# A diffusion trunk on one Trainium2 core: last tile's evictions on two engines behind the first products' copies, its stores on another queue, block sums split elsewhere and combined on GpSimd

## The chip, the core and the metric

The program runs on one core of a Trainium2 chip. The core has a matrix engine (TensorE, written PE in the profile), a vector engine (VectorE, DVE), a scalar engine (ScalarE, ACT), GpSimd (POOL) and SyncE (SP, which here only issues transfers). Each engine works through its own queue of instructions in order; semaphores order work between engines. Transfers between the chip's memory and the core's on-chip memory (SBUF) are issued from the queues of SP and ACT. Matrix products land in PSUM, from which ACT or DVE copies ("evicts") them.

The metric is the device time of one launch in microseconds. Before the change it was 2740.33 us, the median of three runs that lie between 2739.74 and 2740.53.

## The reference

One trunk layer on 2048 latent tokens of width 1024 (256 context tokens enter only the mixer): a gated recurrence (the mixer), then a gated convolutional feed-forward part, each behind an RMS norm with shift and scale. Cut to what the change touches:

```python
D_MODEL, SEQ, D_FF = 1024, 2048, 2816

def conv_ffn(h, w_up, conv_w, conv_b, w_down):
    u = dwconv(h @ w_up, conv_w, conv_b)           # h: (2048, 1024), w_up: (1024, 5632)
    gate, val = jnp.split(u, 2, axis=-1)
    return (jax.nn.silu(gate) * val) @ w_down

    lat = lat + g1 * yl                            # yl: the mixer's output
    hl = modulate(rmsnorm(lat, norm_g[l, 1]), sh2, sc2)
    lat = lat + g2 * conv_ffn(hl, ffn_w_up[l], ffn_conv_w[l], ffn_conv_b[l], ffn_w_down[l])
    return rmsnorm(lat, final_g)
```

The change lies where the mixer's last rows are normed and the first columns of `h @ w_up` are computed.

## The kernel before

**Numbers.** All data are float32. A matrix that enters a product is first split in two: `split(h, l, src)` has ACT copy the source into a rounded form `h` (line 78) and DVE subtract that from the source, which gives the rest `l` (line 79). A product of two such pairs is computed as high x high, high x low and low x high.

**Block products.** `h @ w_up` is computed with 7 instead of 8 block products (Strassen's scheme in Winograd's form). The tokens are taken in two halves of 8 tiles of 128 rows; half 1 goes first. On the token side stand, for each half, the blocks B11, B21, B22 (inputs), and T1, T2, T3, T4 (differences of blocks); on the weight side A11, A12, A22 and the sums S1 = A21 + A22, S2 = S1 - A11, S3 = A11 - A21, S4 = A12 - S2. Each of the 22 column chunks of a half has a `Pair` object that holds the four weight blocks (two raw loads of 0.5 MB in the buffer `raw`) and their sums. The products are A11 x B11, S2 x T2, S1 x T1, S3 x T3, A12 x B21, S4 x B22, A22 x T4. Each is one call of `acc_mm`: four steps over the inner dimension, three matrix instructions each (lines 1065, 1067, 1068), 12 matrix instructions of 128x128 by 512 columns. The pairs go two by two (`q` = 0, 1), so each kind of product comes as 24 matrix instructions. In the profile the left name is the PSUM tile: `z` for the first pairs' early products, `za`, `zb`, `zc`, `zd` in the main loop; `rB` stands for B11, B21 and B22, `rT` for T1 to T4.

**The products that come early.** `mixer_out` walks through the mixer's 16 tiles backwards (t = 15 to 0). For each it makes the output product and adds it to the latent rows `lat` (line 1209); then `norm_steps` makes the norm: ACT sums the squares (line 1215), DVE and GpSimd make the scale `rs` (lines 74, 75), and DVE applies it, which gives `xn` (line 1218). `norm2` then transposes `xn` on PE (line 120, 8 transposes), evicts the two PSUM tiles `tp` with shift and scale into `hm` (`transpose_mod`: line 124 on ACT, line 127 on DVE), makes the differences of this tile and its neighbour (lines 1256, 1257, 1262) and splits and puts them (`put`). Tiles 8 to 15 (half 1) are split into place or put, tiles 0 to 7 (half 0) are put into chip memory (`rhs0...`) for later. Since half 1 is complete long before tile 0 is done, the first two pairs of half 1 (`first`) are begun in here, so that PE has work while tile 0 is normed: A11 x B11 (result copied to `u2` by ACT, line 1345), A12 x B21 (added to it in PSUM, copied to `ug` by ACT, line 1351) and S2 x T2 (added to `u2` by DVE, line 1366). The rest of these pairs, S1 x T1, S4 x B22, S3 x T3 and A22 x T4, is the start of the main loop. There DVE adds S1 x T1 to `u2`, which gives `uv` (line 1549), S4 x B22 goes onto the same PSUM tile `zd`, and S3 x T3 is added to `uv` (line 1557).

**Weights of the first pairs.** S1 and S2 are made by DVE (`sums`, lines 1132, 1133). Since their buffers are needed again, `sums_in_place` writes S3 and S4 with DVE over A21 and A12 (lines 1139, 1140) and copies S1 with ACT over A11 (line 1141); S1 is split from there. For all later pairs GpSimd makes S1 to S4 (lines 1132, 1133, 1149, 1153; the same line can show on either engine).

**Buffers.** The buffers of T3 and T4 (`rT3`, `rT4`, tiles of 2 MB) lie on memory that the mixer uses up to the transposes of tile 0; they are loaded by SP (line 1108), T3 first. The loads of the next raw weights (line 1095) come behind them in SP's queue. Weight splits go into a ring of 11 buffers; the buffers of two earlier states (`Sf`, `Sb`) serve besides.

**What sets the order.** The program's text gives the order of the calls; a scheduler then sets the order on each engine by priority (text order, unless `tc.high_priority` moves a piece ahead), with ties: `tc.issue_after(i)` holds what is issued inside it behind instruction i, and `behind_of(pair)` behind the two instructions of a split. `prepare(g)` issues the weight splits of the main loop's g-th product ahead of its use; how far ahead is set by the `while ready <= ...` line.

Of the kernel before, what the change touches and what calls it, by code (L numbers as in the profile page):

```python
# [11 lines left out]
F32 = mybir.dt.float32  # L12
F32R = mybir.dt.float32r
# [32 lines left out]
def body(ctx, tc, a, out):  # L46
# [1073 lines left out]
    class Pair:  # L1120
# [14 lines left out]

        def sums_in_place(self):

            v = self.src
            dve.tensor_tensor(v["A21"], v["A11"], v["A21"], OP.subtract)
            dve.tensor_tensor(v["A12"], v["A12"], v["S2"], OP.subtract)  # L1140
            act.activation(v["A11"], v["S1"], AF.Copy)
            self.src = {"S3": v["A21"], "S4": v["A12"], "S1": v["A11"], "A22": v["A22"]}

        def split(self, n, w=None):
            if n in self.w:
                return
            if n == "S3" and n not in self.src:
                s3 = self.src["A21"]
                pool.tensor_tensor(s3, self.src["A11"], s3, OP.subtract)
                self.src[n] = s3  # L1150
            if n == "S4" and n not in self.src:
                s2 = self.src["S2"]
                pool.tensor_tensor(s2, self.src["A12"], s2, OP.subtract)
                self.src[n] = s2
            if w is None:
                w = ring_tile([128, 2, 4, 128])
            split(w[:, 0], w[:, 1], self.src[n])
            self.w[n] = w
# [5 lines left out]
    def mixer_out(c3):  # L1164
# [57 lines left out]
        def put(n, t, src):  # L1222
# [13 lines left out]
            put_split.append(split(w[:, 0], w[:, 1], src))  # L1236
            (sp if t > 1 else act).dma_start(rhs_d[half][n][:, j], w.bitcast(F32))

        def norm2(t, xn, on_act=True):

            hm = wn.tile([128, KT, 128], F32, name="hm", tag="hm", bufs=3)
            for g in range(2):
                transpose_mod(xn, hm, g, ps, A2, B2, "tr", 4, on_act)
            a, b = hm[:, 0:4], hm[:, 4:8]
# [91 lines left out]
        for q, p in enumerate(first):  # L1336
            p.sums(dve, *[pl[1][:, q, i].bitcast(F32) for i in range(2)])
        for q, p in enumerate(first):
            p.split("S2", pl[0][:, 2 + q])
        al = []  # L1340
        for q, p in enumerate(first):
            z = ps.tile([128, HJ, 128], F32, name="z", tag="y")
            multiplied = acc_mm(z, p.w.pop("A11"), rhs["B11"], True)
            u2 = h2p.tile([128, HJ, 128], F32, name="u2", tag="u2", bufs=2)
            act.activation(u2, z, AF.Copy)
            al.append((z, u2))
        for q, p in enumerate(first):
            z, u2 = al[q]
            acc_mm(z, p.w.pop("A12"), rhs["B21"], False)
            ug = u_tile(h2p, "g")  # L1350
            kept = act.activation(cols(ug, 0), z, AF.Copy).ins
            begun.append((u2, ug))
            if q == 0:
                for p in first:
                    p.sums_in_place()
                for p in first:
                    p.split("S1")
        behind.append(tc.cur_priority)
        with tc.issue_after(kept), tc.issue_after(multiplied):
            norm2(0, xn)  # L1360
        for q, p in enumerate(first):
            u2, _ = begun[q]
            z = ps.tile([128, HJ, 128], F32, name="z", tag="oi")
            acc_mm(z, p.w.pop("S2"), rhs["T2"], True)
            with tc.issue_after(put_split[2 * q - 4][1]):
                dve.tensor_tensor(u2, u2, z, OP.add)
# [154 lines left out]

    with tc.high_priority(offset=tc.cur_priority - behind[0]):
        for g in range(4):
            prepare(g)
    ready, added = 4, []
    for g, (half, s, n, q, pairs) in enumerate(todo):
        with ExitStack() as tied:
            for i in added[-1:]:
                tied.enter_context(tc.issue_after(i))
            while ready <= min(g + LOOK, max(2 * g + 3, 5)):  # L1530
                prepare(ready)
                ready += 1
# [332 lines left out]
```

## Time and profile before

| what | value |
|---|---|
| median of three runs | 2740.33 us |
| the profiled execution, its own time | 2739.58 us |
| its span (first to last instruction) | 2737.9 us |
| mean granted TensorE clock | 0.997 |
| busy PE | 2702.6 us, 99% |
| busy DVE | 1978.3 us, 72% |
| busy ACT | 1138.8 us, 42% |
| busy GpSimd | 566.8 us, 21% |
| PE busy from 1485 to 1490 us | 3.84 of 5.00 us |
| PE busy from 1490 to 1495 us | 2.27 of 5.00 us, granted clock 0.67 |

A time such as 1470.43 is counted in microseconds from the first instruction. The place of the change is the stretch from about 1465 to 1530 us of this span. A row of a timeline gives start, duration, engine, line, operation, output <- inputs, sizes and count; in brackets how long the engine was idle before it and what ended that. A row of a table of windows gives, for a stretch, the busy time and number of instructions of PE, of its weight loads, of DVE, ACT and GpSimd, then the granted clock of PE, the busy share of the DMA engines and GB/s. In the table of waits a row names the engine and instruction that waited, what it waited for, the total, the number of times, and the longest.

### The profile page before, as it was taken

The numbers are of one execution on the slowest core, as the hardware profiler recorded it, in microseconds if no ns is written. First come the engines' busy times: TensorE is split into PE (matmuls) and PEld (weight loads), VectorE is DVE, ScalarE is ACT, GpSimd is POOL, SyncE is SP. The second block draws the span as 40 slices with busy tenths as digits, with TensorE's granted clock in tenths as the row PEclk, the third lists the DMA queues.
The fourth block names the chain that finished last, engine by engine and source line by source line (L and its number), as shares of the span: only waits on it lengthen the run. The fifth ranks groups of instructions, "written<-read, shape, count | busy, mean of one in ns | idle before, by whom it ended". The sixth has DMA issues, their size and how long they took to land.

```text
span 2737.9 us, 41983 instructions
## 1 busy us (share of the span) xinstructions
PE 2702.6 (99%) x16060; PEld 2254.6 (82%) x16060; DVE 1978.3 (72%) x2799; ACT 1138.8 (42%) x1893; POOL 566.8 (21%) x885
## 2 busy tenths in 40 slices
PE   6999999999999999999999999999999999999999
PEld 4888888888888888888887888888888888888887
DVE  4756655556767776668896887777877787578896
ACT  4434443333233233335666444444544444333444
POOL 2111111011111111211220533443334440000001
PEclk9999999999999999999999999999999999999999
DMA  6313323224544443228888222228322234988653
GB/s 232 93 52 103 104 87 97 85 84 164 168 124 137 149 137 112 85 84 297 295 307 335 93 92 63 89 81 307 92 63 87 83 93 126 312 280 291 197 189 131
DMA packets 229104, 410.56 MB, mean 150 GB/s; under 512 B 29604, under 2 KB 137508, under 8 KB 225064
## 3 DMA queue, kind: packets, MB, share of 16 engines
q1 hardware_dynamic: 223432, 396.03, 44.0%
q10 hardware_dynamic: 5472, 11.86, 1.2%
q8 instruction: 126, 2.06, 0.3%
q14 instruction: 74, 0.61, 0.1%
HBM read 293.23 MB, written 114.57 MB: 149 GB/s over the span
## 4 chain that ended last, share of the span: by engine, by line
PE 94%; DMA 2%; DVE 2%; ACT 1%; issue 1%; POOL 0%; ACTq 0%; SPq 0%; POOLq 0%; DVEq 0%
PE z L449 11%; PE z L451 11%; PE z L450 11%; PE y L1678 5%; PE y L1677 5%; PE y L1679 5%; PE zc L1067 3%; PE zc L1068 3%; PE zc L1065 3%; PE zd L1065 3%; PE zd L1067 3%; PE zd L1068 3%; PE za L1067 3%; PE za L1065 3%; PE za L1068 3%; PE kv L678 2%
## 5 line engine op out<-in xcount | busy, mean ns | idle before, releaser
L449 PE MATMUL z<-tok,w 128*128 128x512 f32 x1280 | 515.3, 403 | 0.0
L451 PE MATMUL z<-tok,w 128*128 128x512 f32 x1280 | 501.1, 391 | 0.0
L450 PE MATMUL z<-tok,w 128*128 128x512 f32 x1280 | 500.8, 391 | 0.0
L79 DVE TENSOR_TENSOR w<-raw,w 128x512 fp32r<-128x512 f32 (+1 forms) x260 | 242.0, 934 | 140.6 <-ACT w L78 136.8
L451 PEld LDWEIGHTS z<-tok,w 128*128 128x128 f32 x1280 | 240.4, 188 | 51.9
L449 PEld LDWEIGHTS z<-tok,w 128*128 128x128 f32 x1280 | 240.7, 188 | 46.0 <-issue 1.7
L450 PEld LDWEIGHTS z<-tok,w 128*128 128x128 f32 x1280 | 241.1, 188 | 45.0 <-DVE tok L79 0.9
L78 ACT ACTIVATE w<-raw 128x512 fp32r<-128x512 f32 (+1 forms) x260 | 196.2, 759 | 140.4 <-PE zd L1068 72.1
L1678 PE MATMUL y<-w,mh 128*128 128x512 f32 x600 | 233.5, 389 | 0.3 <-DVE w L79 0.3
L1679 PE MATMUL y<-w,ml 128*128 128x512 f32 x600 | 233.4, 389 | 0.0
L1677 PE MATMUL y<-w,mh 128*128 128x512 f32 x600 | 233.2, 389 | 0.0
L521 DVE TENSOR_TENSOR_SCAN S<-F,d 128x528 f32<-128x528 f32 (+1 forms) x80 | 91.6, 1145 | 120.5 <-ACT F L503 120.5
L79 DVE TENSOR_TENSOR w<-s,w 128x512 fp32r<-128x512 f32 x126 | 120.8, 964 | 51.3 <-ACT w L78 50.5
L75 POOL TENSOR_TENSOR rs<-rs,mhalf 128x1 f32<-128x1 f32 (+3 forms) x53 | 58.5, 1104 | 423.7 <-DVE rs L74 423.7
L1068 PE MATMUL zc<-rT,w 128*128 128x512 f32 x352 | 136.9, 389 | 0.0
L1065 PE MATMUL zc<-rT,w 128*128 128x512 f32 x352 | 136.9, 389 | 0.0
L1067 PE MATMUL zc<-rT,w 128*128 128x512 f32 x352 | 136.9, 389 | 0.0
L78 ACT ACTIVATE w<-s 128x512 fp32r<-128x512 f32 x126 | 78.3, 628 | 138.4 <-POOL s L1133 80.1
L1678 PEld LDWEIGHTS y<-w,mh 128*128 128x128 f32 x600 | 112.6, 188 | 24.0 <-DVE w L79 0.7
L1679 PEld LDWEIGHTS y<-w,ml 128*128 128x128 f32 x600 | 112.6, 188 | 23.5
L1677 PEld LDWEIGHTS y<-w,mh 128*128 128x128 f32 x600 | 112.6, 188 | 23.4 <-ACT w L78 0.3
L1065 PE MATMUL za<-rB,w 128*128 128x512 f32 x336 | 130.7, 389 | 0.0
(360 smaller groups left out, 6257.6 us busy)
## 6 DMA issues: line engine op xcount, KB each, us to landing
raw<-in_w_up_dram SPq DMA_DIRECT2D x88, 512.0 KB, 4.0
raw<-in_w_in_dram SPq DMA_DIRECT2D x80, 512.0 KB, 4.0
lr<-m SPq DMA_DIRECT2D x49, 512.0 KB, 5.0
m<-r SPq DMA_DIRECT2D x66, 256.0 KB, 3.9
spare<-in_w_ada_dram SPq DMA_DIRECT2D x32, 512.0 KB, 4.1
kq<-stash SPq DMA_DIRECT2D x15, 1024.0 KB, 7.8
og<-stash SPq DMA_DIRECT2D x30, 512.0 KB, 5.5
u<-in_w_down_dram SPq DMA_DIRECT2D x51, 256.0 KB, 3.8
```

What stands on the lines that cost most here:

```text
L78: i = act.activation(h, src, AF.Copy)
L79: j = dve.tensor_tensor(l, src, h.bitcast(F32), OP.subtract)
L449: pe.matmul(z, w[:, 0, k], h, start=k == 0, stop=False, skip_group_check=True)
L450: pe.matmul(z, w[:, 0, k], l, start=False, stop=False, skip_group_check=True)
L451: pe.matmul(z, w[:, 1, k], h, start=False, stop=k == KT - 1, skip_group_check=True)
L521: dve.tensor_tensor_scan(flat(S[:, d]), flat(F[:, d]), flat(d1[:, 0:ns]), 0.0, OP.mult, OP.max)
L1065: pe.matmul(o, w[:, 0, k], r[:, :, 0, k], start=start and k == 0, stop=False, skip_group_check=True)
L1067: pe.matmul(o, w[:, 0, k], r[:, :, 1, k], start=False, stop=False, skip_group_check=True)
L1068: i = pe.matmul(o, w[:, 1, k], r[:, :, 0, k], start=False, stop=k == 3, skip_group_check=True)
L1677: pe.matmul(z, lh, rh, start=start, stop=False, skip_group_check=True)
L1678: pe.matmul(z, lh, rl, start=False, stop=False, skip_group_check=True)
L1679: pe.matmul(z, ll, rh, start=False, stop=stop, skip_group_check=True)
```

## The change

`sums_in_place` is removed. S3 and S4 of the first pairs are now made by GpSimd (`sum3`, line 1138; `sum4`, line 1143), written over A21 and A12 as before, and S1 is split straight from where it was summed: no copies by ACT, no subtractions by DVE. The split S1 of pair 0 goes into the buffer `Sf`, that of pair 1 into the ring.

`norm2` is parted in `norm2_hm` (transposes and evictions) and `modulated2` (differences, splits, puts). For tile 0 the first PSUM tile is evicted by ACT and the second by DVE, right behind the copies of A11 x B11 into `u2` and ahead of the splits of S2 and S1 and of the copies into `ug`; before, ACT evicted both, behind all of these. The puts of tile 0 are issued from SP's queue instead of ACT's. The S2 x T2 products are tied behind A12 x B21, the additions of S2 x T2 to `u2` behind the last split of tile 0, and the main loop's first `prepare` calls as well. The main loop prepares up to 3 products ahead at its start instead of 5.

What this does to the queues, in the scheduled program (names carry a buffer number; `x4` means four in a row):

ACT around tile 0's evictions (`hm` <- `tp`), before: `w_14299` <- `w_14300` are the high parts of S2, `raw_14123` <- `w_14300` the copies of S1, `w_14365` and `w_14368` the high parts of S1.

```order
L78 ACTIVATE w_14299<-w_14300 128x512 x2
L1345 ACTIVATE u2_14328<-z_14315 128x512
L1345 ACTIVATE u2_14343<-z_14330 128x512
L1141 ACTIVATE raw_14123<-w_14300 128x512
L78 ACTIVATE w_14365<-raw_14123 128x512
L1141 ACTIVATE raw_14123<-w_14300 128x512
L78 ACTIVATE w_14368<-raw_14123 128x512
L1351 ACTIVATE ug_14357<-z_14315 128x4x128
L1351 ACTIVATE ug_14383<-z_14330 128x4x128
L124 ACTIVATE hm_14385<-tp_14386,B2_11941,A2_11940 128x128 x4
L124 ACTIVATE hm_14385<-tp_14395,B2_11941,A2_11940 128x128 x4
L78 ACTIVATE w_14301<-hm_14385 128x512 x2
```

The same place now:

```order
L1349 ACTIVATE u2_14324<-z_14311 128x512
L1349 ACTIVATE u2_14339<-z_14326 128x512
L124 ACTIVATE hm_14341<-tp_14342,B2_11941,A2_11940 128x128 x4
L78 ACTIVATE w_14299<-w_14300 128x512 x2
L78 ACTIVATE w_14368<-w_14300 128x512
L78 ACTIVATE w_14371<-w_14300 128x512
L1367 ACTIVATE ug_14386<-z_14311 128x4x128
L78 ACTIVATE w_14301<-hm_14341 128x512 x2
```

The four evictions that are left on ACT moved ahead of the S2 and S1 splits, the copies of S1 are gone, and the other four evictions are on DVE.

GpSimd at the same place, before (`rs` is the scale of a tile's norm, the second one that of tile 0; the rest are edges of the convolution):

```order
L75 TENSOR_TENSOR rs_14197<-rs_14197,mhalf_109 128x1
L75 TENSOR_TENSOR rs_14294<-rs_14294,mhalf_109 128x1
L1395 MEMSET ug_14383 128x1
L1395 MEMSET uv_14497 128x1
L1396 COPY bnd_14467<-ug_14357 128x2
```

And now:

```order
L75 TENSOR_TENSOR rs_14197<-rs_14197,mhalf_109 128x1
L1138 TENSOR_TENSOR raw_14123<-raw_14123 128x512
L75 TENSOR_TENSOR rs_14294<-rs_14294,mhalf_109 128x1
L1143 TENSOR_TENSOR raw_14123<-raw_14123,w_14300 128x512
L1138 TENSOR_TENSOR raw_14123<-raw_14123 128x512
L1143 TENSOR_TENSOR raw_14123<-raw_14123,w_14300 128x512
```

One of the four new sums stands ahead of the scale of tile 0 and one right behind it.

DVE around the additions that give `uv` (the `w` <- `raw` rows are the low parts of weight splits for products from S4 x B22 on), before:

```order
L1366 TENSOR_TENSOR u2_14343<-u2_14343,z_14436 128x512
L79 TENSOR_TENSOR w_14472<-raw_14123,w_14472 128x512
L79 TENSOR_TENSOR w_14475<-raw_14123,w_14475 128x512
L79 TENSOR_TENSOR w_14478<-raw_14123,w_14478 128x512
L79 TENSOR_TENSOR w_14481<-raw_14123,w_14481 128x512
L1549 TENSOR_TENSOR uv_14497<-u2_14328,zd_14484 128x4x128
L1549 TENSOR_TENSOR uv_14512<-u2_14343,zd_14499 128x4x128
```

And now:

```order
L79 TENSOR_TENSOR w_14470<-raw_14123,w_14470 128x512
L1378 TENSOR_TENSOR u2_14324<-u2_14324,z_14420 128x512
L1378 TENSOR_TENSOR u2_14339<-u2_14339,z_14434 128x512
L1561 TENSOR_TENSOR uv_14489<-u2_14324,zd_14476 128x4x128
L79 TENSOR_TENSOR w_14473<-raw_14123,w_14473 128x512
L79 TENSOR_TENSOR w_14491<-raw_14123,w_14491 128x512
L79 TENSOR_TENSOR w_14494<-raw_14123,w_14494 128x512
L1561 TENSOR_TENSOR uv_14510<-u2_14339,zd_14497 128x4x128
```

One split instead of four stands ahead of the first `uv`. On PE the four matrix instructions of S2 x T2 that stood between the transposes and A12 x B21 now come behind A12 x B21, and six of the next pairs' A11 x B11 now stand between S4 x B22 and S3 x T3.

SP's queue at this place, before:

```order
L1108 DMA rT1_14289<-rhs1T1_11958 128x4096
L1108 DMA rT3_14468<-rhs1T3_11959 128x4096
L1108 DMA rT4_14470<-rhs1T4_11962 128x4096
L1095 DMA raw_14123<-in_w_up_dram 128x1024 x8
L1424 DMA m10_11965<-r_14646 128x4x128
```

And now:

```order
L1108 DMA rT1_14289<-rhs1T1_11958 128x4096
L1235 DMA rhs0B11_11949<-w_14301 128x1024
L1235 DMA rhs0B21_11953<-w_14301 128x1024
L1235 DMA rhs0T1_11951<-w_14301 128x1024
L1235 DMA rhs0T2_11950<-w_14301 128x1024
L1235 DMA rhs0T4_11955<-w_14302 128x1024
L1095 DMA raw_14123<-in_w_up_dram 128x1024
L1108 DMA rT3_14466<-rhs1T3_11959 128x4096
L1108 DMA rT4_14468<-rhs1T4_11962 128x4096
L1095 DMA raw_14123<-in_w_up_dram 128x1024 x7
```

The five puts of tile 0 and one load of raw weights now stand ahead of the loads of T3 and T4.

The diff:

```diff
-        def sums_in_place(self):
-
-            v = self.src
-            dve.tensor_tensor(v["A21"], v["A11"], v["A21"], OP.subtract)
-            dve.tensor_tensor(v["A12"], v["A12"], v["S2"], OP.subtract)
-            act.activation(v["A11"], v["S1"], AF.Copy)
-            self.src = {"S3": v["A21"], "S4": v["A12"], "S1": v["A11"], "A22": v["A22"]}
+        def sum3(self):
+            s3 = self.src["A21"]
+            pool.tensor_tensor(s3, self.src["A11"], s3, OP.subtract)
+            self.src["S3"] = s3
+
+        def sum4(self, into):
+            s4 = self.src[into]
+            pool.tensor_tensor(s4, self.src["A12"], self.src["S2"], OP.subtract)
+            self.src["S4"] = s4
...
-            (sp if t > 1 else act).dma_start(rhs_d[half][n][:, j], w.bitcast(F32))
-
-        def norm2(t, xn, on_act=True):
+            (act if t == 1 else sp).dma_start(rhs_d[half][n][:, j], w.bitcast(F32))
+
+        def norm2(t, xn):
+
+            modulated2(t, norm2_hm(xn, (True, True)))
+
+        def norm2_hm(xn, on_act):
 
             hm = wn.tile([128, KT, 128], F32, name="hm", tag="hm", bufs=3)
             for g in range(2):
-                transpose_mod(xn, hm, g, ps, A2, B2, "tr", 4, on_act)
+                transpose_mod(xn, hm, g, ps, A2, B2, "tr", 4, on_act[g])
+            return hm
+
+        def modulated2(t, hm):
+
             a, b = hm[:, 0:4], hm[:, 4:8]
...
-        for q, p in enumerate(first):
-            p.split("S2", pl[0][:, 2 + q])
         al = []
         for q, p in enumerate(first):
             z = ps.tile([128, HJ, 128], F32, name="z", tag="y")
             multiplied = acc_mm(z, p.w.pop("A11"), rhs["B11"], True)
             u2 = h2p.tile([128, HJ, 128], F32, name="u2", tag="u2", bufs=2)
-            act.activation(u2, z, AF.Copy)
+            kept = act.activation(u2, z, AF.Copy).ins
             al.append((z, u2))
+        with tc.issue_after(multiplied), tc.issue_after(kept):
+            hm = norm2_hm(xn, (True, False))
+        for q, p in enumerate(first):
+            with tc.issue_after(kept) if q else ExitStack():
+                p.split("S2", pl[0][:, 2 + q])
+        for p in first:
+            p.sum4("A12")
+        for p in first:
+            p.sum3()
+        p1 = hp.tile([128, 2, 4, 128], F32R, name="w", tag="Sf", bufs=1)
+        for q, p in enumerate(first):
+            p.split("S1", None if q else p1)
         for q, p in enumerate(first):
             z, u2 = al[q]
-            acc_mm(z, p.w.pop("A12"), rhs["B21"], False)
+            multiplied = acc_mm(z, p.w.pop("A12"), rhs["B21"], False)
             ug = u_tile(h2p, "g")
-            kept = act.activation(cols(ug, 0), z, AF.Copy).ins
+            act.activation(cols(ug, 0), z, AF.Copy)
             begun.append((u2, ug))
-            if q == 0:
-                for p in first:
-                    p.sums_in_place()
-                for p in first:
-                    p.split("S1")
+        modulated2(0, hm)
         behind.append(tc.cur_priority)
-        with tc.issue_after(kept), tc.issue_after(multiplied):
-            norm2(0, xn)
+        behind.append(put_split[-1])
         for q, p in enumerate(first):
             u2, _ = begun[q]
             z = ps.tile([128, HJ, 128], F32, name="z", tag="oi")
-            acc_mm(z, p.w.pop("S2"), rhs["T2"], True)
-            with tc.issue_after(put_split[2 * q - 4][1]):
+            with tc.issue_after(multiplied):
+                acc_mm(z, p.w.pop("S2"), rhs["T2"], True)
+            with tc.issue_after(put_split[-1][1]):
                 dve.tensor_tensor(u2, u2, z, OP.add)
...
-    with tc.high_priority(offset=tc.cur_priority - behind[0]):
+    with tc.high_priority(offset=tc.cur_priority - behind[0]), behind_of(behind[1]):
...
-            while ready <= min(g + LOOK, max(2 * g + 3, 5)):
+            while ready <= min(g + LOOK, max(2 * g + 3, 3)):
```

More of the change, by code (lines that the diff above doesn't have):

```diff
@@ L1147, in split @@
             if n == "S3" and n not in self.src:
-                s3 = self.src["A21"]
-                pool.tensor_tensor(s3, self.src["A11"], s3, OP.subtract)
-                self.src[n] = s3
+                self.sum3()
             if n == "S4" and n not in self.src:
-                s2 = self.src["S2"]
-                pool.tensor_tensor(s2, self.src["A12"], s2, OP.subtract)
-                self.src[n] = s2
+                self.sum4("S2")
             if w is None:
```

## The prediction

> **What bounds the kernel now.** I read the page first: the span, the busy time, the shares of the chain that ended last.
>
> ```profile
> span 2737.9 us, 41983 instructions
> PE 2702.6 (99%) x16060; PEld 2254.6 (82%) x16060; DVE 1978.3 (72%) x2799; ACT 1138.8 (42%) x1893; POOL 566.8 (21%) x885
> PE 94%; DMA 2%; DVE 2%; ACT 1%; issue 1%; POOL 0%; ACTq 0%; SPq 0%; POOLq 0%; DVEq 0%
> ```
>
> PE is busy 99% of the span, so another engine's time counts only where PE waits for it. The number of products does not change; what can be won is PE's idle time around the edit. So next the table of PE's waits, its two rows from this place:
>
> ```profile
> PE zd L1065 <- DVE uv L1549: 3.9, 1, 3.9
> PE z L1065 <- ACT w L78: 0.7, 1, 0.7
> ```
>
> S4 x B22 (`zd`) waits once, 3.9 us, for the addition that makes `uv`; S2 x T2 (`z`) waits 0.7 us for the split of S2. The timeline of PE gives the whole loss:
>
> ```profile
> 1465.67 0.39 PE L1065 MATMUL z<-rB,w 128*128 128x512 f32 x1
> ...
> 1470.20 0.40 PE L1068 MATMUL z<-rB,w 128*128 128x512 f32 x1
> 1470.43 1.04 PE L120 MATMUL tp<-ident,xn 128*128 128x128 f32 x8
> 1471.23 0.48 PE L1065 MATMUL z<-rT,w 128*128 128x512 f32 x1
> ...
> 1472.65 0.50 PE L1065 MATMUL z<-rT,w 128*128 128x512 f32 x1 [0.72 <-ACT w L78]
> ...
> 1473.22 0.42 PE L1065 MATMUL z<-rB,w 128*128 128x512 f32 x1
> ...
> 1488.45 0.39 PE L1068 MATMUL zd<-rT,w 128*128 128x512 f32 x1
> 1492.73 0.76 PE L1065 MATMUL zd<-rB,w 128*128 128x512 f32 x1 [3.89 <-DVE uv L1549]
> ...
> 1498.41 0.43 PE L1067 MATMUL zd<-rB,w 128*128 128x512 f32 x1
> ...
> 1500.97 0.39 PE L1065 MATMUL zc<-rT,w 128*128 128x512 f32 x1
> ```
>
> The first two rows are 20 matrix instructions apart: 0.2265 us each at full pace. From the transposes (1470.43) to S3 x T3 (1500.97) PE does 8 transposes (0.80, to 1471.23) and four kinds of 24 products, 96 x 0.2265 = 21.74. Without a wait S3 x T3 would start at 1492.97; it starts 8.0 us later. The parts: four S2 x T2 instructions take 1471.23 to 1473.22, 1.08 more than 4 x 0.2265; the pause before 1492.73 is 4.05 beyond the pace; the 24 of S4 x B22 take 8.24 instead of 5.44, 2.80 more. The table of windows gives the reason of the last:
>
> ```profile
> 1470.00:1475.00 5.00, 4.28 (x23) 3.24 (x22) 5.00 (x10) 2.77 (x6) 0.00 (x0) 1.00 1.01 396
> 1490.00:1495.00 5.00, 2.27 (x6) 1.82 (x6) 4.38 (x8) 2.17 (x4) 0.00 (x0) 0.67 1.06 377
> ```
>
> After the pause of 4.05 the granted clock falls (0.67 over the window), and to 1498.41 the products come 0.43 apart; after the 1.08 it stayed at 1.00. So a wait here costs more than itself once it nears 4 us. 8.0 us, 0.29%, is also the most the change can win. The Trainium skill, "TensorE: Matmul & The Clock Gate", Part 1, has half rate after an idle window of about 3.4 us and full rate after about 3.4 us of busy time. Its two states agree with these rows, its length does not: the slow stretch here is 5.7 us, and by the page 1.7 instead of 2.80 would be lost to it.
>
> Why does `uv` come so late? ACT and DVE:
>
> ```profile
> 1478.81 0.63 ACT L78 ACTIVATE w<-raw 128x512 fp32r<-128x512 f32 x1 [3.19 <-DMA rhs0T<-w]
> 1480.30 2.90 ACT L124 ACTIVATE hm<-tp,B,A 128x128 f32<-128x128 f32 x8
> 1487.83 0.95 ACTq L1237 DMA_DIRECT2D rhs0T<-w  x2
> 1488.83 2.19 ACT L78 ACTIVATE w<-raw 128x512 fp32r<-128x512 f32 x4 [1.23 <-DVE w L79]
> 1489.49 2.50 DVE L79 TENSOR_TENSOR w<-raw,w 128x512 fp32r<-128x512 f32 x4 [0.49 <-ACT w L78]
> 1491.90 1.28 DVE L1549 TENSOR_TENSOR uv<-u,zd 128x512 f32<-128x512 f32 x2
> ```
>
> The transposes were done at 1471.5, but ACT evicts them at 1480.30, behind splits, copies and a wait for a put. Everything of tile 0 follows, then four weight splits (1488.83, 1489.49), and only behind them in DVE's queue the first `uv`.
>
> **The change part by part.**
>
> *What goes.* ACT loses two copies of S1 (0.55 each by the pace of the splits above, 2.19 / 4) and four of eight evictions (2.90 / 2 = 1.45); DVE loses four subtractions. These lie on the path above; their worth is in the waits, not added again. S2 x T2 moves behind A12 x B21: its split is then ready 5.4 us before use (24 x 0.2265), and the 1.08 goes.
>
> *Evictions earlier.* The four on DVE cost, by DVE's only row of this kind,
>
> ```profile
> 213.72 1.37 DVE L127 TENSOR_SCALAR hm<-tp,A,B 128x128 f32<-128x128 f32 x4 [0.82 <-PE tp L120]
> ```
>
> 1.37, beside 1.45 on ACT. They start with the transposes, and tile 0's differences, splits and puts run under A12 x B21 and S2 x T2 instead of under S1 x T1. `uv` then has one split ahead of it instead of four. The first half of S1 x T1 ends 60 products after the transposes; the first `uv`, 0.64 long, follows, and S4 x B22 wants it 12 products (2.7 us) after that. Cover 2.1 us; if it is gone, each us DVE is late is a us of PE, between 0 and the 4.05 of before. I take 0: the 4.05 and with it the 2.80 go.
>
> *Sums on GpSimd.* The four are like the first row here; what stands at the transposes and what the two engines do to each other:
>
> ```profile
> 1510.72 1.29 POOL L1132 TENSOR_TENSOR s<-raw 128x512 f32<-128x512 f32 x1
> 1511.82 1.28 DVE L1412 SCALAR_TENSOR_TENSOR r<-uv,conv,r 128x1023 f32<-128x1023 f32 x1 [1.31 <-ACT r L1408]
> 1512.08 2.19 POOL L1133 TENSOR_TENSOR s<-s,raw 128x512 f32<-128x512 f32 x1
> 1513.03 1.79 DVE L79 TENSOR_TENSOR w<-raw,w 128x512 fp32r<-128x512 f32 x1
> 1465.09 0.68 DVE L1132 TENSOR_TENSOR w<-raw 128x512 f32<-128x512 f32 x1
> 1466.39 0.69 DVE L79 TENSOR_TENSOR w<-hm,w 128x512 fp32r<-128x512 f32 x1
> 1468.49 0.85 POOL L75 TENSOR_TENSOR rs<-rs,mhalf 128x1 f32<-128x1 f32 x1 [8.55 <-DVE rs L74]
> 1469.38 0.75 DVE L1218 TENSOR_SCALAR xn<-lat,rs 128x1024 f32<-128x1024 f32 x1 [0.43 <-POOL ug L1395]
> ```
>
> The sum at 1512.08 takes 2.19 instead of 1.29, since DVE's work on SBUF runs to 1513.1; then DVE's split takes 1.79 instead of 0.69 until the sum ends. One waits out the other. S3 of pair 0 can start when S1 is there (1465.77) and holds to 1467.06, so DVE's split of 1466.39 and all behind it, the scale of tile 0 too, come 0.67 later: `xn` at 1470.05. S4 of pair 0 stands right behind the scale on GpSimd and is free at nearly the same time. If it is first, `xn` waits 1.25 more, ends at 1472.0, and the transposes start there instead of at 1470.43: 1.6 lost. If `xn` is first, it ends at 1470.9: 0.4 lost. I take 1.6, since S4 needs no signal from another engine at that moment; the range keeps 0.4. The other two sums hold DVE at most 2.5 us more, under A12 x B21.
>
> The Trainium skill, "SBUF — State Buffer", section "SBUF: two separate sides", calls this an exclusive lock held for the whole instruction, and includes DVE operations in a two-port mode. The rows agree for operations with two SBUF inputs; none shows `xn`, which has one. Were `xn` free of it, 0.7 would be lost instead of 1.6.
>
> *Stores and loads.* The five puts leave ACT's queue, where they cost it issue time, for SP's, ahead of the loads of T3 and T4. The loads:
>
> ```profile
> 1477.93 10.86 SPq L1108 DMA_DIRECT2D rT<-rhs1T  x2
> rT<-rhs1T SPq DMA_DIRECT2D x3, 2048.0 KB, 10.6
> rhs0B<-w ACTq DMA_DIRECT2D x3, 512.0 KB, 3.0
> rB<-rhs0B SPq DMA_DIRECT2D x1, 2048.0 KB, 7.8
> raw<-in_w_up_dram SPq DMA_DIRECT2D x4, 512.0 KB, 8.8
> raw<-in_w_up_dram SPq DMA_DIRECT2D x88, 512.0 KB, 4.0
> ```
>
> T3 was issued at 1477.93. Now it waits in the queue for the last put and one raw load. From eviction (1480.30) to the last puts (1487.83) went 7.5 us; now the evictions start near 1472.5, save 1.45, and have the S1 and S2 splits in between (4 x 0.63 on DVE) and the two sums (2.5): 1483.6 for the last put, and 2 us more until the split that frees the raw buffer is done (four operations of 0.5 to 0.6 on either engine): T3 issued at 1485.6. Alone such a load takes 7.8 (fourth row); with two 0.5 MB puts beside it 10.6 (second row, T1's), 1.4 for each. With three small transfers ahead it takes 7.8 to 7.8 + 4.2; half of that is over when it is issued, at best. T3 lands between 1495.5 and 1497.6, in the middle 1496.6. T4, 2 MB more, follows 4 x 1.4 = 5.6 later (1502.2); it is wanted 24 products and four hoisted ones behind S3 x T3 (1502.9).
>
> *Order on PE.* Six of the next pairs' products come before S3 x T3: no cost, 1.36 more time for T3. The smaller look-ahead moves S3's split behind `uv`; it has 8 us until use.
>
> **Sum.** PE: 1472.0 + 0.80 + 102 x 0.2265 (23.10) = 1495.9 for S3 x T3. Before, with six more products ahead, it would be 1500.97 + 1.36 = 1502.33. The gain is 1502.33 minus the later of 1495.9 and the landing: 6.4 with 1495.5, 5.7 with 1496.6, 4.7 with 1497.6. If `xn` comes first, PE is there at 1494.8, and the landing alone decides. So 5.7, against the profiled execution's own 2739.58 (span and 1.68 around it): 2733.9. That execution is 0.75 below the median of the runs; from the median it would be 2734.6. I say 2734.2, between them.
>
> **The rivals.**
>
> - *T3 is the new wait.* The three transfers ahead count in full or more, or tile 0's puts are later by a us or two; T3 lands from 1497.6 to 1499.5. For: 7.7 us later issue, second row above. Against: the memory traffic falls afterwards. Gain 4.7 to 2.8: 2735 to 2737.5.
> - *The gain comes back behind it.* T4 and seven raw loads come after T3, 1.4 each, to 1512; the next pairs' sums on GpSimd and splits come that much later than before. For: the cover for T4 is 0.7 us. Against: before, this stretch ran without a PE wait over 0.1 us with raw loads of 8.8 us. Two or three us lost: 2737.5 to 2740.
> - *Slower.* T3 and T4 share the engines instead of going one after the other, 4 MB instead of 2 before T3 is whole: 1496.6 + 5.6 = 1502.2. PE then pauses 6.3, which by the row of 1492.73 brings the half clock, 2.8; with 1.6 at the transposes 10.7 are lost against 8.0: 2742.3; if T4's splits and raws fall behind too, to 2748. It decides once T3 lands after 1499.5 (1.6 + a pause of 3.6 + 2.8 = 8.0). Against: 0.5 MB raw loads issued right behind T4's took 8.8 instead of 4.0 (last two rows), as in a line, not shared. The Trainium skill's page "TensorE: Matmul & The Clock Gate" would halve the clock from 3.4 us of pause on, at a landing of 1499.3; the rows show only that 1.08 does not do it and 4.05 does.
>
> **How the numbers follow.** Chances: forecast, with the variant in which `xn` is first and T3 early (up to 7.5, 2732.1), 0.50; T3 as the new wait 0.26; the gain comes back 0.11; slower 0.13, of which about half ends past 0.2%. 0.2% is 5.5 us, 2734.85 and 2745.8, about what a measurement of this kernel tells from no change. So faster 0.50, same 0.43, slower 0.07. The forecast's own range is 2732.4 to 2735.0; with T3 as the new wait and the nearer part of the third case the range is 2732.4 to 2738.5, which leaves out about 2 in 10.
>
> **What would show it.** The table of PE's waits has no `zd` behind `uv`; the granted clock stays at 1.00 from 1490 to 1500; the transposes start near 1472.0, with GpSimd's sum over 1470 to 1471.3; `hm` is evicted by two engines within 3 us of it; T3's load is issued near 1485.6 and `zc` waits for it under 2 us. I am wrong if PE has a wait over 2 us for `rT`, or if a wait of `z` or `zd` for DVE is left, which would mean that the sums hold DVE longer than four times 1.25.

## The result

The changed kernel takes 2735.07 us (median of 17 runs, 2732.25 to 2737.41) against 2740.53 before (17 runs, 2739.06 to 2743.32): 5.46 us less, a ratio of 0.998 with a 95% interval of 0.9973 to 0.9986. It is faster, by almost exactly the 0.2% that the prediction had set as the bound between a gain and no change. Predicted were 2734.2 and a range of 2732.4 to 2738.5.

The profiled execution of the changed kernel took 2736.98, 1.9 above its median, and its span is only 2.6 us shorter. So the comparison is made inside the stretch. Two measures serve for it and for the experiments, both counted from the end of the last A11 x B11 instruction:

- M: to the first instruction of S3 x T3, without instructions hoisted in between. Before 30.54, after 24.70, without any wait 22.54.
- L: what PE loses until the end of the first pairs' last A22 x T4 instruction, beyond 0.80 us for the transposes and 0.2267 us for each product in between. Before 7.99.

The two waits of PE between 1465 and 1700 us, in the table of waits of the changed kernel:

```profile
PE tp L120 <- DVE xn L1216: 1.3, 1, 1.3
PE zc L1065 <- DMA rT<-rhs1T: 0.3, 1, 0.3
```

The 3.9 us for `uv` and the 0.7 us for S2's split are gone; in their place stand a wait of the transposes for `xn` and a short one for T3's load. PE's timeline of the changed kernel:

```profile
1471.35 0.39 PE L1068 MATMUL z<-rB,w 128*128 128x512 f32 x1
1473.09 1.09 PE L120 MATMUL tp<-ident,xn 128*128 128x128 f32 x8 [1.35 <-DVE xn L1216]
...
1497.64 0.50 PE L1065 MATMUL zc<-rT,w 128*128 128x512 f32 x1 [0.30 <-DMA rT<-rhs1T]
...
1509.51 0.39 PE L1068 MATMUL zc<-rT,w 128*128 128x512 f32 x1
```

and the end of the same stretch before, where the first product after A22 x T4 starts:

```profile
1511.85 0.39 PE L1065 MATMUL za<-rB,w 128*128 128x512 f32 x1
```

After: 1471.58 to 1509.74 is 38.16 us with 154 products (ten hoisted) and the transposes: L = 38.16 - 0.80 - 34.91 = 2.45. Before: 1470.43 to 1511.86 with 144 products: L = 41.43 - 0.80 - 32.64 = 7.99. The difference, 5.54, is the 5.46 that the medians show. From there to the products of the last part the two profiles take the same time to 0.2 us. The rest of the difference between the two spans lies elsewhere: the stretch began 1.15 later, and the last part took 1.6 longer; over the profiles of this case its start moves between 1469.4 and 1472.1 and the last part between 426.4 and 430.8 (426.4 to 428.1 in those made from the kernel before), so this can be chance and was not followed further.

The table of windows of the changed kernel, at the two places that had a half clock before:

```profile
1490.00:1495.00 5.00, 5.00 (x24) 4.14 (x23) 3.69 (x6) 2.27 (x4) 0.00 (x0) 1.00 1.04 412
1495.00:1500.00 5.00, 4.70 (x21) 3.59 (x20) 4.48 (x5) 3.02 (x4) 0.10 (x1) 1.00 1.02 436
```

The clock is 1.00 in both (0.67 before in the first): with the long pause its aftermath is gone too.

How the transposes came late is seen on GpSimd and DVE of the changed kernel:

```profile
1467.04 1.31 POOL L1138 TENSOR_TENSOR raw<-raw 128x512 f32<-128x512 f32 x1 [5.96 <-DMA lat<-lat]
1467.52 1.38 DVE L79 TENSOR_TENSOR w<-hm,w 128x512 fp32r<-128x512 f32 x1
1470.31 0.85 POOL L75 TENSOR_TENSOR rs<-rs,mhalf 128x1 f32<-128x1 f32 x1 [1.96 <-DVE rs L74]
1471.21 1.27 POOL L1143 TENSOR_TENSOR raw<-raw,w 128x512 f32<-128x512 f32 x1
1471.20 1.83 DVE L1216 TENSOR_SCALAR xn<-lat,rs 128x1024 f32<-128x1024 f32 x1 [0.44 <-POOL rs L75]
```

The sum S3 held DVE's split (1.38 instead of 0.69), and S4 won against `xn` by less than the resolution of the record: both start within 0.01, S4 takes its usual 1.27 and `xn` 1.83 instead of 0.75. The Trainium skill's rule on the port pair ("SBUF — State Buffer", section "SBUF: two separate sides") counts DVE operations in a two-port mode in. The row of `xn`, which has one SBUF input, agrees with it if `xn` runs in such a mode, which no row here tells.

Evictions, `uv` and T3's load:

```profile
1473.78 1.50 ACT L124 ACTIVATE hm<-tp,B,A 128x128 f32<-128x128 f32 x4 [1.41 <-PE tp L120]
1475.99 1.36 DVE L127 TENSOR_SCALAR hm<-tp,A,B 128x128 f32<-128x128 f32 x4
1487.86 0.69 DVE L1561 TENSOR_TENSOR uv<-u,zd 128x512 f32<-128x512 f32 x1 [0.65 <-PE zd L1068]
1487.11 1.70 SPq L1108 DMA_DIRECT2D rT<-rhs1T  x2
```

`uv` now waits for PE, not PE for `uv`: it is done at 1488.55, and S4 x B22 begins 72 products after 1473.94, at 1490.37. T3 and T4 are issued from 1487.11 on.

### The profile page after: what moved, and what is told of

Its sections match the earlier page's. It is cut to its first block, busy times and chain, and to the rows that moved or that the text cites. A ratio compares the mean times of both kernels' runs of the same rounds, so it can differ in the third digit from the quotient of the medians.

```text
span 2735.3 us, 41983 instructions
## 1 busy us (share of the span) xinstructions
PE 2703.1 (99%) x16060; PEld 2253.8 (82%) x16060; DVE 1977.5 (72%) x2799; ACT 1135.7 (42%) x1887; POOL 572.7 (21%) x889
## 4 chain that ended last, share of the span: by engine, by line
PE 90%; DVE 4%; DMA 3%; issue 1%; ACT 1%; POOL 1%; SPq 0%; ACTq 0%; POOLq 0%; DVEq 0%
PE z L451 11%; PE z L449 11%; PE z L450 11%; PE y L1690 4%; PE y L1691 4%; PE y L1689 4%; PE zc L1065 3%; PE zc L1068 3%; PE zc L1067 3%; PE zd L1068 3%; PE zd L1065 3%; PE zd L1067 3%; PE za L1068 3%; PE za L1067 3%; PE za L1065 3%; PE kv L678 2%
```

## The experiments

All runs in one table; the gain is against the median of the kernel before on the same chip.

| run | products between | L | us, median | difference to before | ratio, 95% interval |
|---|---|---|---|---|---|
| before | 144 | 7.99 | 2740.53 | | |
| whole change | 154 | 2.45 | 2735.07 | -5.46 | 0.9973 to 0.9986 |
| eviction early, alone | 144 | 9.52 | 2742.23 | +1.48 | 0.9998 to 1.0015 |
| smaller look-ahead, alone | 144 | 6.02 | 2738.36 | -2.39 | 0.9983 to 1.0002 |
| eviction all on ACT | 154 | 1.70 | 2734.78 | -5.97 | 0.9969 to 0.9987 |
| puts on ACT's queue | 149 | 2.50 | 2735.42 | -5.33 | 0.9972 to 0.9990 |
| sums on DVE | 151 | 1.24 | 2734.40 | -5.31 | 0.9971 to 0.9989 |
| sums behind `xn` | 154 | 2.26 | 2735.49 | -4.22 | 0.9977 to 0.9995 |
| T3 and T4 early | 144 | 13.53 | 2747.09 | +7.38 | 1.0018 to 1.0040 |
| both of the last two | 144 | 13.44 | 2747.77 | +8.06 | 1.0018 to 1.0039 |
| sums on DVE, T3 behind the puts | 144 | 1.30 | 2734.57 | -6.14 | 0.9970 to 0.9987 |
| T4 ahead of T3 | 156 | 11.15 | 2746.50 | +5.79 | 1.0010 to 1.0030 |
| eviction early, T3 and T4 behind puts | 144 | 5.27 | 2739.41 | -1.30 | 0.9988 to 1.0006 |
| T3 behind the puts, eviction on ACT | 144 | 0.82 | 2735.11 | -5.60 | 0.9970 to 0.9989 |

L comes from one profile of each kernel; how far it moves from one execution of a kernel to the next was not measured. L less 7.99 agrees with the difference of the medians to within 2.7 us. L also ends too early for six of the runs: with the smaller look-ahead alone, in the run with the eviction and the puts, and in all four with the raw loads held behind T3 and T4, PE waits once more behind it, 0.55 to 0.57 for a split of the next pairs, and its way to the products of the last part is 0.8 to 0.9 us longer than before. The changed kernel gives 0.2 back there, the others nothing.

**Eviction early, alone.** The kernel before with:

```diff
+        with tc.issue_after(multiplied), tc.issue_after(copied):
+            hm = norm2_hm(xn, (True, False))
+        for q, p in enumerate(first):
+            with tc.issue_after(copied):
+                p.split("S2", pl[0][:, 2 + q])
...
-            norm2(0, xn)
+            modulated2(0, hm)
```

> The kernel before with one part of the change alone: tile 0's PSUM tiles are evicted on two engines right behind the copies into u2, and the splits of S2 come behind these. Sums, puts, ties and look-ahead stay as before. Measure M: from the end of the last A11 x B11 instruction to the first S3 x T3 instruction, without instructions hoisted between them; before 30.54 us, ideal 22.54, after the whole change 24.70. My theory (uv was late because the evictions stood behind splits and copies): the wait of zd for uv falls below 1 us, the clock stays at 1.00, nothing holds xn, M between 22.6 and 24.0, so 6.5 to 8 us faster than before and 1 to 2 faster than the whole change. Rival (the sums, puts and the smaller look-ahead are what frees ACT and DVE): M stays above 28, less than 2.5 us faster than before.

Measured: M 26.76, L 9.52, no gain. Neither theory: `uv` comes earlier, but not enough (2.38 of the pause is left), and a second pause, of 3.58, appears between S3 x T3 and A22 x T4. PE, ACT and DVE of this run, and its transfers:

```profile
1489.37 0.67 PE L1065 MATMUL zd<-rB,w 128*128 128x512 f32 x1 [2.22 <-DVE uv L1560]
...
1505.53 0.47 PE L1065 MATMUL zc<-rT,w 128*128 128x512 f32 x1 [3.42 <-issue]
```
```profile
1496.48 1.16 ACT L78 ACTIVATE w<-raw 128x512 fp32r<-128x512 f32 x2 [8.83 <-DMA rhs0T<-w]
1497.14 1.29 DVE L79 TENSOR_TENSOR w<-raw,w 128x512 fp32r<-128x512 f32 x2 [7.32 <-ACT w L78]
...
1504.74 0.68 DVE L1568 TENSOR_TENSOR uv<-uv,zc 128x512 f32<-128x512 f32 x1
```
```profile
rhs0T<-w ACTq DMA_DIRECT2D x4, 512.0 KB, 12.3
```

ACT stands 8.83 us in front of two splits until a put of tile 0 has landed (issued at 1483.31, landed at 1496.40). In the order of the program these are the splits of A22: those of S4 and S3 are the four ahead of `uv`, and S3 x T3 began at 1496.51 without a wait. DVE's halves of the two splits stand 7.32 us with them, and behind these in DVE's queue comes the addition of S3 x T3 to `uv` (1504.74), which must have read the PSUM tile `zc` before A22 x T4 is computed onto it. PE's row says `issue`, since the profile names no releaser; in the trace PE waits for a semaphore that DVE raises at 1505.44, with this addition, and goes on at 1505.53. The puts take 12.3 us to land here, against 4.4 in the changed kernel:

```profile
rhs0T<-w SPq DMA_DIRECT2D x3, 512.0 KB, 4.4
```

because T3 and T4 (4 MB) are issued at 1476.58 and 1483.95, ahead of or among the puts (1480.3 to 1484.4). The queue is not the reason: in the run with the puts on ACT's queue below, where both loads come behind them, they land in 3.9. Alone, then, the early eviction is no gain.

**Eviction early, with the puts ahead of the loads.** The same kernel, and

```diff
-            (sp if t > 1 else act).dma_start(rhs_d[half][n][:, j], w.bitcast(F32))
+            stored.append((act if t == 1 else sp).dma_start(rhs_d[half][n][:, j],
+                                                            w.bitcast(F32)).ins)
...
+    with tc.issue_after(stored[-1]):
         for n in ("T3", "T4"):
             load_rhs(1, n)
```

> The kernel before with two parts of the change: the early eviction on two engines, and tile 0's puts in SP's queue with T3's and T4's loads behind them. The early eviction alone gave L 9.52. My theory (alone it failed because T3's and T4's 4 MB went ahead of the puts whose landing frees the buffers of S3's splits): the wait of S3's splits for a put goes, S3 x T3 waits for T3 itself between 0 and 2.5 us, the clock stays full, L 0.5 to 3, 5 to 7.5 us faster than before. Rival (the sums on DVE and ACT make it slow): a wait of zd or zc for a split or for uv of over 2 us stays, L above 5.

Measured: L 5.27, 1.30 us faster, an interval that includes no change. The splits of A22 (of S3, as the expectation has it, they are not) now stand 1.53 us at most, at no cost to PE, and the wait for `uv` is gone (the scheduler now puts the splits behind it). L is above 5, as the rival had it, but neither splits nor `uv` make it so. What is left is one wait for T3, longer than I gave it, and its aftermath; PE and its window of this run:

```profile
1495.55 0.47 PE L1065 MATMUL zc<-rT,w 128*128 128x512 f32 x1 [3.28 <-DMA rT<-rhs1T]
```
```profile
1495.00:1500.00 5.00, 4.45 (x13) 3.54 (x14) 1.70 (x2) 1.63 (x2) 0.10 (x1) 0.67 0.97 409
```

T3 lands no earlier, counted from A11 x B11, than in the changed kernel (26.1 and 26.0 us), but PE is there sooner: nothing holds its transposes, and no product of the next pairs is hoisted ahead. The whole change loses 1.51 at the transposes and spends 1.36 on hoisted products in the time in which this one stands still and falls to half clock.

**T3 and T4 early in the changed kernel.** The puts back on ACT's queue, the raw loads behind both loads:

```diff
-            (act if t == 1 else sp).dma_start(rhs_d[half][n][:, j], w.bitcast(F32))
+            (sp if t > 1 else act).dma_start(rhs_d[half][n][:, j], w.bitcast(F32))
...
-        load_rhs(1, n)
+        turned = load_rhs(1, n).ins
...
-    with tc.high_priority(offset=tc.cur_priority - behind[0]), behind_of(behind[1]):
+    with tc.high_priority(offset=tc.cur_priority - behind[0]), behind_of(behind[1]), \
+            tc.issue_after(turned):
```

> The changed kernel with T3's and T4's loads first in SP's queue (puts of tile 0 on ACT's queue, raw loads behind the two loads). My theory: T3 lands 7 to 9 us earlier than it is needed, PE's wait for it (0.46 us) goes, M 24.2; nothing else moves. Rival (the raw loads that now come later than T3 and T4 hold up the splits of S3 and A22): zc waits for a split by 1 us or more, M above 25.5.

Measured: 7.38 us slower than before, L 13.53. T3 itself is early (it landed at 1490.38, 5.6 us before S3 x T3, where I expected 7 to 9), and M is 24.24. But then the same wait as with the eviction alone, and longer; ACT and DVE of this run, and PE behind them:

```profile
1502.41 0.63 ACT L78 ACTIVATE w<-raw 128x512 fp32r<-128x512 f32 x1 [12.16 <-DMA rhs0T<-w]
1503.07 0.69 DVE L79 TENSOR_TENSOR w<-raw,w 128x512 fp32r<-128x512 f32 x1 [11.07 <-ACT w L78]
...
1510.06 0.68 DVE L1571 TENSOR_TENSOR uv<-uv,zc 128x512 f32<-128x512 f32 x1
```
```profile
1510.84 0.76 PE L1065 MATMUL zc<-rT,w 128*128 128x512 f32 x1 [9.29 <-issue]
```

A put and not a raw load ends ACT's wait, so it is not the rival's wait either.

**Puts on ACT's queue, alone.** Only the first two lines of that diff.

> The changed kernel with tile 0's five puts issued from ACT's queue as before; T3's load then stands behind one raw load only. My theory: T3 is issued up to 1 us earlier and three small transfers are not all ahead of it, PE does not wait for T3, M 24.3 (0.4 less than the whole change); the puts' issue on ACT delays splits by 1 to 2 us but uv has 2 us of cover. Rival (the puts on ACT were what made uv late): zd waits for uv or for a split by over 1 us, M above 25.7.

Measured: M 24.92, L 2.50, 5.33 us faster than before, as the whole change. T3's load stands behind one raw load, which is issued at 1483.70 when a split has freed its buffer, and by then the puts are out (1479.42 to 1483.64). So the move of the puts to SP's queue pays nothing by itself; that T3's load comes behind the puts, by whichever queue, is what is needed. My 0.4 less did not come: PE still waits 0.53 for T3.

**T4 ahead of T3.**

```diff
-    for n in ("T3", "T4"):
+    for n in ("T4", "T3"):
```

> The changed kernel with T4's load ahead of T3's: T3 lands behind 2 MB more. It prices a late T3 and the pause after which the clock is halved. If the queue works in line, T3 lands 5 to 6 us later than in the changed kernel and PE pauses 5 to 6.5 us; with the half clock of the row before (2.8) L goes from 2.45 to 10 to 11.5, some 8 us slower than the changed kernel. If transfers of one queue share the bandwidth, T3 lands hardly later than now (T4 lands at the same time), and L stays below 4.

Measured: L 11.15, 5.79 us slower than before. PE of this run:

```profile
1502.55 0.79 PE L1065 MATMUL zc<-rT,w 128*128 128x512 f32 x1 [3.36 <-DMA rT<-rhs1T]
...
1516.53 0.50 PE L1065 MATMUL zc<-rT,w 128*128 128x512 f32 x1 [2.40 <-DVE uv L1569]
```

S3 x T3 starts 30.5 us after A11 x B11 (1472.07) instead of 26.1: 2 MB ahead in the same queue cost 4.4 us, so the queue works in line. The pause is only 3.5, since the scheduler hoisted six more products; the half clock then took 2.9, and a second wait for `uv` 2.4 that I had not seen. The sum was right, its parts were not.

**Sums on DVE.** `sum3` and `sum4` of the first pairs with `dve.tensor_tensor` in the changed kernel.

> The changed kernel with S3 and S4 of the first pairs made by DVE, as before, instead of GpSimd. M counts as in the other runs (before 30.54, whole change 24.70). My theory (GpSimd's sums hold DVE's split and then xn): PE does not wait for xn, the transposes start with the end of A11 x B11, M 23.2 to 23.7, 1.0 to 1.5 us less than the whole change. Rival (DVE has no room for four more operations): xn is on time but uv or a split comes late, zd or z waits over 1 us, M 24.7 or more.

Measured: M 23.67, L 1.24. PE of this run:

```profile
1469.80 1.03 PE L120 MATMUL tp<-ident,xn 128*128 128x128 f32 x8
...
1494.15 0.50 PE L1065 MATMUL zc<-rT,w 128*128 128x512 f32 x1 [0.86 <-DMA rT<-rhs1T]
```

The transposes start with no wait, and DVE has the room. L is 1.21 less than with the whole change; the wait for T3 is longer (0.86 instead of 0.30) and takes back part of the 1.51. In the medians (5.31 less than before) it cannot be told from the whole change.

**Sums behind `xn`.** GpSimd keeps them, but later:

```diff
+        seen = wn.tile([128, 1], F32, name="seen", tag="seen", bufs=1)
+        with tc.issue_after(pool.tensor_copy(seen, xn[:, 0:1]).ins):
+            for p in first:
+                p.sum4("A12")
+            for p in first:
+                p.sum3()
```

> The changed kernel with GpSimd's four sums held behind xn: one column of xn is copied on GpSimd, and the sums stand behind that copy. My theory: no operation on GpSimd holds DVE ahead of xn, so PE does not wait at the transposes (1.5 us less); all of tile 0 comes 1 to 1.5 us earlier, T3's load too, and PE still waits for T3 between 0.4 and 1.0: M 23.3 to 24.2. Rival (the sums only cost DVE elsewhere): the wait returns at z or zd, M unchanged.

Measured: M 24.68, L 2.26, 4.22 us faster than before. The rival was nearly right: the transposes start at once, and most of the 1.5 us come back. PE of this run:

```profile
1496.81 0.50 PE L1065 MATMUL zc<-rT,w 128*128 128x512 f32 x1 [1.07 <-DMA rT<-rhs1T]
```

1.07 for T3, 0.5 in S2 x T2 for a split. T3 is issued 15.9 us after A11 x B11 instead of 15.5: the four sums now hold DVE just behind `xn`, where S2's second sum, a split and the first difference of tile 0 take 1.80, 1.79 and 1.76 instead of 0.69 each.

**Both of these.** T3 and T4 early and the sums behind `xn`.

> The changed kernel with both: sums held behind xn, and T3's and T4's loads first in SP's queue. My theory: both waits of the changed kernel go, M 22.6 to 23.0, 7.5 to 8 us less than before and about 2 less than the whole change. Rival (the waits replace each other): M stays at 24 or more.

Measured: M 23.50, above the 22.6 to 23.0 of my theory (PE waits 0.48 in S2 x T2 for a split), L 13.44, 8.06 us slower than before. It goes like the run with T3 and T4 early, for the same reason.

**Smaller look-ahead, alone.** The kernel before with `max(2 * g + 3, 3)`.

> The kernel before with the smaller look-ahead alone (3 products instead of 5 at the start of the main loop): two of the four weight splits that stood ahead of uv in DVE's queue come behind it. My theory: uv comes 1.2 us earlier (two splits of 0.6), the pause of zd falls from 4.05 to about 2.8; whether the half clock still comes is open, M 29.3 with it, 26.5 without. Rival (the splits ahead of uv are the whole cause, evictions do not matter): the pause is gone, M under 24.5.

Measured: M 28.58, L 6.02; 2.39 us faster, at an interval that just includes no change. The pause falls from 4.05 to 3.14, and the half clock still comes, though later; PE of this run:

```profile
1491.09 0.47 PE L1065 MATMUL zd<-rB,w 128*128 128x512 f32 x1 [2.99 <-DVE uv L1549]
...
1492.58 0.63 PE L1065 MATMUL zd<-rB,w 128*128 128x512 f32 x1
```

L falls by 1.97 without touching the evictions, about a third of the whole change's 5.54, but 0.9 is lost again behind its end, and the medians do not tell the gain from none. The rival, that the splits ahead of `uv` are the whole cause, is out.

**Eviction all on ACT.** The changed kernel with `norm2_hm(xn, (True, True))`.

> The changed kernel with tile 0's evictions all on ACT again (8 instead of 4), at the changed, early place. My theory (the place matters, the second engine little): ACT needs 1.45 us more, tile 0's puts and T3's load come up to 1.4 us later, PE waits for T3 up to 1.4 us more: M 24.7 to 26.1. Rival (two engines are what pays): the wait of zd for uv is back with over 2 us, M above 27.

Measured: M 24.24, L 1.70, 5.97 us faster than before: no loss at all. In the changed kernel DVE starts its four only at 1475.99, behind two sums and a split held by GpSimd, when ACT has ended (1473.78 + 1.50). The place of the evictions matters (alone it brought M from 30.54 to 26.76), the second engine does not.

**T3 directly behind the puts,** with the sums on DVE, and the raw loads behind T3 and T4 (the last two pieces of the diff of T3 and T4 early):

> The kernel of the run with the sums on DVE, and besides T3's and T4's loads directly behind tile 0's puts in SP's queue, with all raw loads behind them. Measure L: what PE loses from the end of A11 x B11 to the end of the first pairs' last A22 x T4, beyond 0.80 us for the transposes and 0.2267 us for each product between; before 7.99, whole change 2.45, sums on DVE 1.24. My theory (T3 should come behind the puts, since the buffers of the next splits are freed by them, but ahead of the raw loads): T3 is issued about 0.7 us earlier with 0.5 MB less ahead of it, its wait of 0.86 goes, L 0.3 to 0.6, 7.4 to 7.7 less than before. Rival (T3 early holds up what comes behind it, as in the two slower runs): a wait for a split or a raw load of 1 us or more comes, L above 1.5.

Measured: 2734.57, 6.14 us less than before. PE's wait for T3 falls to 0.41, a second one of 0.22 for T4 appears, and one of 0.56 for a split of the next pairs, beyond the end of L. L is 1.30, where I expected 0.3 to 0.6: what T3 gains T4 gives back, and the next pairs lose more behind L.

**The same, with the evictions all on ACT:**

> As the run with T3 behind the puts (sums on DVE), but with tile 0's evictions all on ACT. My theory (the second engine is not what pays): L within 0.7 us of that run. Rival: four more evictions on ACT delay the splits of S2 and S1 and the puts, L more than 1 us above it.

Measured: L 0.82, 2735.11, 5.60 us less than before; in PE's waits of the stretch only the 0.56 is left. Of the 7.99 this leaves 0.82, the lowest L; with what comes behind it 1.7 are lost, 2.2 in the run before this one, 2.6 in the changed kernel and 1.2 in the one with the sums on DVE. Yet the gains of these last two kernels and of the changed one lie within 0.7 us of each other, less than their intervals tell apart. No version was shown to beat the changed kernel.

## Why the prediction was right, and where its reasons were not

**The sum.** The gain was put at 5.7, as 1502.33 minus the later of PE's arrival and T3's landing. Counted from the end of A11 x B11, S3 x T3 was to start 26.2 us after it, and started 26.06 after it. From the medians 5.46 came.

**Sums on GpSimd.** 1.6 was taken, with S4 ahead of `xn`; 1.51 was measured, in that order. How much of it could be had was shown by the runs without it: 1.21 of L with the sums on DVE, 0.19 with the sums behind `xn`, since T3's load comes next. The prediction's formula has this in it (the landing alone decides if `xn` comes first).

**Stores and loads.** T3 was to be issued 15.2 us after A11 x B11 (1485.6 - 1470.43) and was at 15.5; to land at 26.2, landed at about 26.0; PE's wait was to be 0.7, and was 0.46. T4 landed at 1504.04 of the changed kernel's profile and was wanted at 1504.11: of the 0.7 us of cover 0.1 was there. That T3's issue came within 0.3 of the sum is in part luck, since one of its terms was not there (see the two engines).

**Evictions earlier.** This is the step whose reason failed: "I take 0: the 4.05 and with it the 2.80 go" rested on the place of the evictions and on one split instead of four ahead of `uv`. The 4.05 did go in the whole change, but the early eviction alone left 2.38 of the pause and the smaller look-ahead alone 3.14. The eviction also brought a new pause of 3.58 that I had not named: the splits of A22 wait for tile 0's puts, which T3's and T4's loads hold up, and DVE's addition to `uv` waits behind them. I had looked at who waits for the loads, and not at who waits for the puts. So the loads' place behind the puts, which the prediction treated as the price of the change, is a condition of its gain. How the gain is shared between the eviction, the look-ahead and the ties stays open: the two were not run together without the rest, and their effects do not add up (+1.53 and -1.97 of L against -5.54).

**On two engines.** The sum of T3's issue had 1.45 taken off for the second engine. That term was not there: with all eight on ACT T3 is issued 15.47 us after A11 x B11, in the changed kernel 15.53. DVE's four started 2.2 us behind ACT's there, when ACT was about to be free.

**The rivals.** T3 as a new wait came with 0.46, within the forecast and not as the rival. The late T3 of the slower rival was made by an experiment: with 2 MB ahead it starts 4.4 us later, not 5.6. Loads of one queue go in line, as the 8.8 us of the raw loads had suggested.

## What to carry to other kernels

When work is moved ahead of a wait, list not only what it waits for, but also who waits for the buffers it uses: a store that frees a buffer is a dependency like any other, and large loads issued around it delayed it here even from another queue, to 12.3 and 17.3 us instead of about 4. Where one engine stands against several waits that end within a few us, taking one away alone wins what lies between it and the next (here 1.5 us turned into 1.2 and 0.2, and the early eviction alone into a loss). Count a stretch's lost time on the bounding engine: it shows which wait a difference of 1 us comes from, where medians with a spread of 4 us show nothing. Let the stretch end where the kernels run alike again, and remember that it is one execution.

## What was not expected of the hardware

**The clock.** The prediction knew that a pause of 1.08 leaves the clock and one of 4.05 halves it. The runs give the points between, and they do not form a sharp bound: 1.51 and less, no half clock; 2.38 (eviction alone), half clock for 8 products; 2.56 (T4 first, the second wait), none; 3.14 to 3.58, in all four cases, for 8 to 14 products. What the products behind it lose beyond the pause lies between 1.7 and 2.9 us (2.4 and 2.1 after the pauses of 9.5 and 10.4). It need not begin with the end of the pause: in the run with the smaller look-ahead the first six products came at full pace, and the slow ones 1.5 us later. The Trainium skill ("TensorE: Matmul & The Clock Gate", Part 1) speaks of a window of about 3.4 us that runs freely. That 2.38 halved the clock and 2.56 did not agrees with a free window, in which the place of a pause would decide; its length does not agree, since 2.38 is less than one window.

**Transfers.** With 4 MB of loads on SP's queue and 2.5 MB of puts on ACT's, a put of 0.5 MB took 12.3 us, and 17.3 in the run with T3 and T4 early, instead of 4.4. At the 414 to 420 GB/s of the first run's windows from 1485 to 1495, the 6.5 MB take about 16 us by my estimate. There T4, issued at 1483.95, landed at 1494.89, and the puts issued from 1481.51 to 1484.43 landed from 1493.02 to 1497.99: a small transfer in the other queue did not get past a large one, even one issued behind it.
